# The heads' stage of a hybrid streaming step: masks written behind the last low part of the first gates' weights, the values' low parts on VectorE, signs on ScalarE

## The chip, the core and the metric

The kernel runs on one core of a Trainium2 chip. The metric is the device time in microseconds (us) of one execution. The engines are TensorE (PE, with its weight loads PEld), VectorE (DVE), ScalarE (ACT), GpSimd (POOL) and SyncE (SP), whose queue issues nearly all transfers.

## The reference

One layer of an encoder for a prompt of 1024 rows and a sample of 64 rows, all in float32. The normalised input goes through one projection, whose columns are split among all groups:

```python
z = xn @ w_in
qa, ka, va, qi, ki, wi, qb, kb, vb, ga, gb = jnp.split(z, SPLIT_POINTS, axis=-1)
```

Two mixers of 8 heads of 64 stand side by side. Mixer A lets each query see only the 256 keys with the best index score (48 in the sample):

```python
s = jax.nn.relu(jnp.einsum('bqhd,bsd->bqhs', q_i, ki_all))
isc = jnp.einsum('bqh,bqhs->bqs', w, s).astype(jnp.float32)
isc = jnp.where(vis[None], isc, -jnp.inf)
_, idx = lax.top_k(isc, topk)
```

Mixer B is a band of the query's own chunk of 64 and the eight before it, with a learned bias. Both are projected, weighted by sigmoid gates from `ga` and `gb`, added, projected, and followed by an MLP.

## The kernel before

**Numbers in two parts.** A float32 operand is split into a high part that PE takes (`hi`, a copy on ACT, L123) and a low part (`lo`, raw minus high). `split` (L143) puts the subtraction on DVE (L146) or on POOL (L148). A product is then three matmuls (high by high, high by low, low by high: L154 to L156), or two (L162, L163) where one side is already exact in stacked form (the sample's rows `xsT`, the index scores `s`).

**Stages.** First come normalisation, index keys and queries, and the index scores: `stage_scores(i)` computes the eight heads' scores of row block i on PE into PSUM banks `s`, and DVE adds them up into `work[i]` (L364, L366). Then `project_heads` (L433) makes the six projections of the heads in the order vb, kb, qb, ka, va, qa. Each first loads eight weight pieces of 128 x 512 (transfer `wraw`, high part `whi`, low part `wlo`, 11 buffers each) and then runs 9 units: for each block of 128 rows 24 matmuls of 512 columns, and for the sample's rows 16. A unit's sum in PSUM is copied to a tile `t` (3 buffers), normed and rotated where it must be (POOL L460 and L220 to L223), split into a tile `pair` (3 buffers) and written out (`keep`, `values_to_dram`, `rows_to_dram`, L417 and L424). The sample's two halves are added at L212 (`fold`).

**Order of the stages.** The generator `heads` is drawn one unit at a time. `stage_scores(NT - 1, ...)` draws one behind head 3 and one behind head 7 of the last prompt block, `stage_scores(NT, ...)` one behind head 7 of the sample's block. The rest follows in one loop once the score banks are given back and made into four `wide` banks (L516). Which bank a unit uses is set by `turn`: the first FIRST (3) draws take `acc` (2 banks), later ones acc, wide, wide in turn. The program as a whole is ordered by a compile-time scheduler that simulates the engines; `tc.issue_after(x)` holds what stands under it behind instruction x.

**The masks.** `choose` (L520) finds, in a search of 31 steps, the threshold of each row of blocks 2 to 7: counts on DVE for blocks 2 to 4 (L531), sign sums on ACT for blocks 5 to 7 (L536). Then come `thr` (L570) and a loop over the six blocks (384 to 1024 columns): the scores' signs are given back (L575), scores over the threshold marked and counted (L576, L577), those equal to it marked (L578), their running number made by a scan (L579), cut at what is still needed (L581) and added (L583), and POOL writes the mask (L584). The tiles `seen` have two buffers, so a block's L578 waits for the mask of the block before.

**Gates and attention.** Behind the heads, eight weight pieces of the first four gate blocks are loaded (L633 to L639, low part on DVE), and 12 gate chunks run on PE (L586 to L594), each copied by ACT to one of two `gate` buffers and written out. Then the pools `tk`, `pj`, `works`, `fw` are closed, and the space that they leave is used for the ring of weights that the attention reads beside its own work (`raw`, `hi`, `lo`, L652) and for the attention's tiles. Attention reduces the scores on DVE (L679), takes exponentials on ACT (L683), scales on POOL (L686) and transposes on PE (L699); the mixer's b heads run first, and the masks are first needed when the a heads begin.

Of the kernel before, what the change touches and what calls it, by code (L numbers as in the profile page):

```python
# [14 lines left out]
AF = mybir.ActivationFunctionType  # L15
ALU = mybir.AluOpType
# [10 lines left out]
HD = 64  # L27
# [5 lines left out]
RING = 5  # L33
FIRST = 3
WARM = 18
# [9 lines left out]
def kernel(  # L45
# [97 lines left out]
    def split(raw, hi, lo, lo_on_vector=False):  # L143
        copy(hi, raw)
        if lo_on_vector:
            nc.vector.tensor_sub(lo, raw, hi)  # L146
        else:
            nc.gpsimd.tensor_sub(lo, raw, hi)  # L148
# [275 lines left out]
    def values_to_dram(t, rows, dst, r0):  # L424
        both = pj.tile([P, TP], F32R, tag="pair", name="pair", bufs=3).rearrange("p (h z d) -> p h z d", h=H, z=2)
        split(t[:rows].rearrange("p (h d) -> p h d", d=HD), both[:rows, :, 0], both[:rows, :, 1])
        nc.sync.dma_start(dst[r0:r0 + rows], both.bitcast(F32)[:rows])
# [54 lines left out]
    stage_scores(NT - 1, {3: heads, 7: heads})  # L482
    stage_scores(NT, {7: heads})
    close_pool("ix")
# [34 lines left out]
    def choose(vector, scalar):  # L519
# [50 lines left out]
        nc.vector.tensor_mul(thr, bits.bitcast(F32), sgn)  # L570
        for j, (i, w) in enumerate(zip(blocks, ws)):
            n = w.shape[1]
            over, same = (tk.tile([P, TP], BF16, tag="seen", name="seen", bufs=2) for _ in range(2))
            nth = tk.tile([P, TP], F32, tag="nth", name="nth", bufs=1)
            nc.vector.tensor_scalar(w, w, col(sgn, j), None, op0=ALU.mult)  # L575
            nc.vector.tensor_scalar(over[:, :n], w, col(thr, j), 0.0, op0=ALU.is_gt, op1=ALU.add, accum_out=col(cnt, j))  # L576
# [6 lines left out]
            nc.vector.tensor_add(over[:, :n], over[:, :n], same[:, :n])  # L583
            nc.gpsimd.tensor_scalar(mask[i], over[:, :n], -1.0, BIG, op0=ALU.add, op1=ALU.mult)  # L584

    def gate(m, ws, after=None):  # L586
# [35 lines left out]
    with tc.issue_after(state["last"].ins):  # L622
# [4 lines left out]
        nc.vector.tensor_scalar(mask_s, work_s, 0.5 * (HIDDEN + TAKEN), -BIG, op0=ALU.is_gt, op1=ALU.mult)  # L627
        choose([2, 3, 4], [5, 6, 7])
    todo = [(mix, h) for mix in "ba" for h in range(H)]
    first_head = load_head(*todo[0], kv)  # L630
    for g in range(0, EARLY, 4):
        ws = []
        for k in range(KB):  # L633
# [4 lines left out]
            split(raw, hi, lo, lo_on_vector=True)  # L638
            ws.append((hi, lo))  # L639
        for q in range(4):  # L640
            gate(g + q, [(h[:, q * P:(q + 1) * P], l[:, q * P:(q + 1) * P]) for h, l in ws])
    for nm in ("tk", "pj", "works", "fw"):
        close_pool(nm)
# [688 lines left out]
```

## Time and profile before

| | us |
|---|---|
| median of 3 runs | 1738.48 (1738.3 to 1742.39) |
| the profiled execution | 1739.78 |
| its span, from the first to the last instruction | 1738.0 |
| PE busy | 1709.3 (98%) |
| DVE busy | 1199.3 (69%) |
| ACT busy | 956.4 (55%) |
| POOL busy | 481.4 (28%) |

The mean granted clock of PE is 0.997 of full speed. Busy shares are averages over stages: an engine that is busy for little of the span can still be the one that PE waits for in one place. Times of single instructions below are counted from the start of the span, in the one profiled execution.

### The profile page before, as it was taken

What the parts mean: (1) busy time and instruction counts of PE and PEld (TensorE: products, weight loads), DVE (VectorE), ACT (ScalarE), POOL (GpSimd) and SP (SyncE); (2) the same over time, 40 slices, a digit from 0 to 9 for tenths busy, and PEclk for the clock granted to TensorE, in tenths of its full rate; (3) what the DMA queues carried; (4) which work ended last, traced back from release to release, by engine and by line L of the source; (5) the groups of instructions that cost most, each with busy time, mean ns of one, the idle gap of its engine ahead of it and who ended that gap; (6) DMA issues with size and microseconds to landing.
All of it is one profiled execution on the core that took longest, in us unless ns stands there. A gap on an engine that the chain in (4) does not pass through costs nothing.

```text
span 1738.0 us, 30914 instructions
## 1 busy us (share of the span) xinstructions
PE 1709.3 (98%) x10540; PEld 1551.3 (89%) x10540; DVE 1199.3 (69%) x2765; ACT 956.4 (55%) x1994; POOL 481.4 (28%) x549
## 2 busy tenths in 40 slices
PE   8999999999999999999999999999999999999999
PEld 6877888877999999999999999999999978888887
DVE  6776799994447777774354345865587658868787
ACT  5785889722357777776443346644454447343430
POOL 2252432545424333332344354000000011111122
PEclk9999999999999999999999999999999999999999
DMA  5022475444667876664544559555566589565643
GB/s 175 8 81 104 149 201 151 152 161 161 180 162 191 198 176 153 159 146 134 170 137 136 185 163 284 168 184 183 186 209 204 165 300 316 183 199 149 199 124 103
DMA packets 277197, 294.97 MB, mean 170 GB/s; under 512 B 39792, under 2 KB 201584, under 8 KB 277040
## 3 DMA queue, kind: packets, MB, share of 16 engines
q1 hardware_dynamic: 248064, 257.61, 51.0%
q10 hardware_dynamic: 28976, 35.40, 5.8%
q8 instruction: 83, 1.36, 0.3%
q14 instruction: 74, 0.61, 0.1%
HBM read 199.85 MB, written 93.08 MB: 169 GB/s over the span
## 4 chain that ended last, share of the span: by engine, by line
PE 85%; DVE 6%; DMA 3%; issue 3%; ACT 2%; POOL 1%; SPq 0%; ACTq 0%; DVEq 0%; POOLq 0%
PE acc L154 9%; PE acc L156 9%; PE acc L155 9%; PE x L156 5%; PE x L155 5%; PE x L154 5%; PE pt L699 4%; PE wide L154 3%; PE wide L155 3%; PE wide L156 3%; PE s L162 3%; PE po L715 2%; PE s L163 2%; PE po L714 2%; PE pg L156 2%
## 5 line engine op out<-in xcount | busy, mean ns | idle before, releaser
L155 PE MATMUL x<-lo,hi 128*128 128x512 f32 x432 | 168.8, 391 | 2.3 <-POOL lo L148 1.7
L156 PE MATMUL x<-hi,lo 128*128 128x512 f32 x432 | 166.8, 391 | 0.0
L154 PE MATMUL x<-hi 128*128 128x512 f32 x432 | 164.2, 392 | 0.0
L148 POOL TENSOR_TENSOR lo<-wr,hi 128x512 fp32r<-128x512 f32 x15 | 35.1, 2343 | 455.6 <-ACT hi L123 455.6
L148 POOL TENSOR_TENSOR lo<-raw,hi 128x512 fp32r<-128x512 f32 x88 | 117.9, 1350 | 153.7 <-ACT hi L123 145.8
L123 ACT ACTIVATE hi<-raw 128x512 fp32r<-128x512 f32 x104 | 64.3, 627 | 90.4 <-PE acc L155 21.6
L711 DVE TENSOR_TENSOR pl<-pt,ph 128x512 fp32r<-128x512 f32 (+4 forms) x184 | 96.6, 545 | 19.5 <-ACT ph L123 18.9
L536 ACT ACTIVATE nth<-work,cand 128x768 bf16<-128x768 f32 (+2 forms) x93 | 96.6, 1039 | 18.3 <-DVE cand L553 14.1
L146 DVE TENSOR_TENSOR lo<-hr,hi 128x512 fp32r<-128x512 f32 x108 | 81.6, 756 | 28.9 <-ACT hi L123 28.7
L155 PEld LDWEIGHTS x<-lo,hi 128*128 128x128 f32 x432 | 81.1, 188 | 21.2 <-POOL lo L148 2.1
L123 ACT ACTIVATE ph<-pt 128x512 fp32r<-128x512 f32 (+4 forms) x184 | 81.6, 483 | 32.4 <-PE pt L699 25.6
L156 PEld LDWEIGHTS x<-hi,lo 128*128 128x128 f32 x432 | 81.1, 188 | 17.9
L154 PEld LDWEIGHTS x<-hi 128*128 128x128 f32 x432 | 81.1, 188 | 17.6
L154 PE MATMUL acc<-xnT,hi 128*128 128x384 f32 (+1 forms) x288 | 95.5, 331 | 0.0
L156 PE MATMUL acc<-xnT,lo 128*128 128x384 f32 (+1 forms) x288 | 94.3, 327 | 0.0
L155 PE MATMUL acc<-xnT,hi 128*128 128x384 f32 (+1 forms) x288 | 94.3, 327 | 0.0
L686 POOL TENSOR_SCALAR mw<-mw,sm 128x640 f32<-128x640 f32 (+1 forms) x64 | 56.7, 886 | 131.8 <-DVE sm L685 131.7
L154 PE MATMUL wide<-whi,xnT 128*128 128x512 f32 x224 | 89.4, 404 | 1.7 <-DVE work_s L366 1.7
L156 PE MATMUL wide<-whi,xnT 128*128 128x512 f32 x224 | 90.1, 402 | 0.0
L155 PE MATMUL wide<-wlo,xnT 128*128 128x512 f32 x224 | 89.9, 401 | 0.0
L714 PE MATMUL po<-ph,vhl 128*128 128x256 f32 (+2 forms) x336 | 86.0, 274 | 0.4 <-ACT ph L123 0.4
L715 PE MATMUL po<-pl,vhl 128*128 128x256 f32 (+2 forms) x336 | 85.9, 285 | 0.6 <-DVE pl L711 0.6
(671 smaller groups left out, 5963.2 us busy)
## 6 DMA issues: line engine op xcount, KB each, us to landing
hr<-h SPq DMA_DIRECT2D x108, 256.0 KB, 3.6
wr<-in_w_down_dram SPq DMA_DIRECT2D x76, 256.0 KB, 4.0
wraw<-in_w_in_dram SPq DMA_DIRECT2D x56, 256.0 KB, 2.8
h<-h ACTq DMA_DIRECT2D x32, 272.0 KB, 2.1
raw<-in_w_out_dram SPq DMA_DIRECT2D x32, 256.0 KB, 3.0
raw<-in_w_up_dram SPq DMA_DIRECT2D x32, 256.0 KB, 3.5
out_dram<-t SPq DMA_DIRECT2D x24, 256.0 KB, 2.4
g_dram<-gate SPq DMA_DIRECT2D x32, 192.0 KB, 3.2
```

The lines of the kernel that those rows point to most:

```text
L123: return nc.scalar.activation(out, in_, AF.Copy)
L146: nc.vector.tensor_sub(lo, raw, hi)
L148: nc.gpsimd.tensor_sub(lo, raw, hi)
L154: nc.tensor.matmul(out, sh, mh, start=(opens and i == 0), stop=False, skip_group_check=resumes)
L155: nc.tensor.matmul(out, sh, ml, start=False, stop=False, skip_group_check=resumes)
L156: last = nc.tensor.matmul(out, sl, mh, start=False, stop=(closes and i == n - 1), skip_group_check=resumes)
L536: nc.scalar.activation(sign[:, :w.shape[1]], w, AF.Sign, bias=against, scale=-1.0, accum_out=col(cnt, j))
L686: nc.gpsimd.tensor_scalar(m[:rows, :n], m[:rows, :n], sm[:rows, 6:7], 1.0, op0=ALU.mult, op1=ALU.mult)
L699: nc.tensor.transpose(ps[:krows, oo:oo + qrows], m[:qrows, kc:kc + krows], ident[:qrows, :qrows])
L711: nc.vector.tensor_sub(pl[:kr, a:b], ps[:kr, a:b], ph[:kr, a:b])
L714: nc.tensor.matmul(dst, vhl[:krows, vt, :], ph[:krows, oo:oo + width], start=(idx == 0), stop=False)
L715: nc.tensor.matmul(dst, vhl[:krows, vt, :], pl[:krows, oo:oo + width], start=False, stop=(idx == n - 1))
```

## The change

Five edits. FIRST goes from 3 to 5, so that the first five units drawn use `acc`. `stage_scores(NT, ...)` draws a unit behind head 3 too. The low parts of the values va are made on DVE, not on POOL (vb stays on POOL). The six multiplications that give the scores back their signs become ACT copies with a scale. The rest of the mask loop becomes a function `mask_out(j)`, which is called for the six blocks behind the gates, under `tc.issue_after` of the low part of the eighth weight piece of the first gates.

```diff
--- before.py
+++ after.py
@@ -31,7 +31,7 @@
 DFF = 4096
 EPS = 1e-6
 RING = 5
-FIRST = 3
+FIRST = 5
 WARM = 18
 BIG = 1e30
 HIDDEN = -2.0e38
@@ -143,7 +143,7 @@
     def split(raw, hi, lo, lo_on_vector=False):
         copy(hi, raw)
         if lo_on_vector:
-            nc.vector.tensor_sub(lo, raw, hi)
+            last["lo"] = nc.vector.tensor_sub(lo, raw, hi)
         else:
             nc.gpsimd.tensor_sub(lo, raw, hi)
 
@@ -423,7 +423,8 @@
 
     def values_to_dram(t, rows, dst, r0):
         both = pj.tile([P, TP], F32R, tag="pair", name="pair", bufs=3).rearrange("p (h z d) -> p h z d", h=H, z=2)
-        split(t[:rows].rearrange("p (h d) -> p h d", d=HD), both[:rows, :, 0], both[:rows, :, 1])
+        split(t[:rows].rearrange("p (h d) -> p h d", d=HD), both[:rows, :, 0], both[:rows, :, 1],
+              lo_on_vector=dst is v_dram["a"])
         nc.sync.dma_start(dst[r0:r0 + rows], both.bitcast(F32)[:rows])
 
     def keep(nm, t, rows, i):
@@ -480,7 +481,7 @@
 
     heads = project_heads()
     stage_scores(NT - 1, {3: heads, 7: heads})
-    stage_scores(NT, {7: heads})
+    stage_scores(NT, {3: heads, 7: heads})
     close_pool("ix")
 
     masks = open_pool("masks")
@@ -568,11 +569,14 @@
         nc.vector.scalar_tensor_tensor(cand.bitcast(F32), low, 1.5 * 2.0 ** -24, low, op0=ALU.mult, op1=ALU.add)
         nc.vector.copy_predicated(bits, ok, cand)
         nc.vector.tensor_mul(thr, bits.bitcast(F32), sgn)
-        for j, (i, w) in enumerate(zip(blocks, ws)):
+        for j, w in enumerate(ws):
+            nc.scalar.activation(w, w, AF.Copy, scale=col(sgn, j))
+
+        def mask_out(j):
+            i, w = blocks[j], ws[j]
             n = w.shape[1]
             over, same = (tk.tile([P, TP], BF16, tag="seen", name="seen", bufs=2) for _ in range(2))
             nth = tk.tile([P, TP], F32, tag="nth", name="nth", bufs=1)
-            nc.vector.tensor_scalar(w, w, col(sgn, j), None, op0=ALU.mult)
             nc.vector.tensor_scalar(over[:, :n], w, col(thr, j), 0.0, op0=ALU.is_gt, op1=ALU.add, accum_out=col(cnt, j))
             nc.vector.tensor_scalar(col(need, j), col(cnt, j), -1.0, float(TOPK_P), op0=ALU.mult, op1=ALU.add)
             nc.vector.tensor_scalar(same[:, :n], w, col(thr, j), None, op0=ALU.is_equal)
@@ -582,6 +586,8 @@
                                            op0=ALU.is_le, op1=ALU.mult)
             nc.vector.tensor_add(over[:, :n], over[:, :n], same[:, :n])
             nc.gpsimd.tensor_scalar(mask[i], over[:, :n], -1.0, BIG, op0=ALU.add, op1=ALU.mult)
+
+        return mask_out
 
     def gate(m, ws, after=None):
         for c0, n in CHUNKS:
@@ -625,7 +631,7 @@
             nc.vector.max(out=m8, in_=work_s)
             nc.vector.match_replace(out=work_s, in_to_replace=m8, in_values=work_s, imm_value=TAKEN)
         nc.vector.tensor_scalar(mask_s, work_s, 0.5 * (HIDDEN + TAKEN), -BIG, op0=ALU.is_gt, op1=ALU.mult)
-        choose([2, 3, 4], [5, 6, 7])
+        mask_out = choose([2, 3, 4], [5, 6, 7])
     todo = [(mix, h) for mix in "ba" for h in range(H)]
     first_head = load_head(*todo[0], kv)
     for g in range(0, EARLY, 4):
@@ -637,8 +643,13 @@
             lo = pj.tile([P, 512], F32R, tag="wlo", name="wlo", bufs=11)
             split(raw, hi, lo, lo_on_vector=True)
             ws.append((hi, lo))
+        lows = last["lo"]
         for q in range(4):
             gate(g + q, [(h[:, q * P:(q + 1) * P], l[:, q * P:(q + 1) * P]) for h, l in ws])
+
+        with tc.issue_after(lows.ins):
+            for j in range(6):
+                mask_out(j)
     for nm in ("tk", "pj", "works", "fw"):
         close_pool(nm)
```

How the order of instructions changes, at three places. First PE at the last score block (`s`, the sample's rows); `acc` and `wide` are projection units. Before:

```order
L162 MATMUL s<-kih,qiT 64x192
L163 MATMUL s<-kil,qiT 64x192
L162 MATMUL s<-kih,qiT 64x192
L163 MATMUL s<-kil,qiT 64x192
L154 MATMUL wide<-whi,xnT 128x512
L155 MATMUL wide<-wlo,xnT 128x512
L156 MATMUL wide<-whi,xnT 128x512
L154 MATMUL wide<-whi,xnT 128x512
```

After:

```order
L162 MATMUL s<-kih,qiT 64x192
L163 MATMUL s<-kil,qiT 64x192
L162 MATMUL acc<-whi,xsT 128x512
L163 MATMUL acc<-wlo,xsT 128x512
L162 MATMUL acc<-whi,xsT 128x512
L163 MATMUL acc<-wlo,xsT 128x512
L162 MATMUL s<-kih,qiT 64x192
L163 MATMUL s<-kil,qiT 64x192
L154 MATMUL acc<-whi,xnT 128x512
L155 MATMUL acc<-wlo,xnT 128x512
L156 MATMUL acc<-whi,xnT 128x512
L162 MATMUL s<-kih,qiT 64x192
```

Before, the eight pairs of narrow matmuls follow on each other and `wide` comes behind them; after, `acc` matmuls stand between the pairs.

Second DVE, at the masks. `thr` is the threshold, `work_111` the scores of the first block (384 columns), `t` tiles of a projection. Before, the masks follow `thr` at once:

```order
L139 TENSOR_TENSOR nt<-nt,ms 128x8
L139 TENSOR_TENSOR nt<-nt,ms 64x8
L569 COPY_PREDICATED bits<-ok,cand 128x6
L140 SCALAR_TENSOR_TENSOR rs<-nt,r_3703 128x8
L140 SCALAR_TENSOR_TENSOR rs<-nt,r_3758 64x8
L570 TENSOR_TENSOR thr<-bits,sgn 128x6
L457 TENSOR_TENSOR t<-wide,rs 128x512
L457 TENSOR_TENSOR t<-fold,rs 64x512
L576 TENSOR_SCALAR seen,cnt<-work_111,thr 128x384
L578 TENSOR_SCALAR seen<-work_111,thr 128x384
L577 TENSOR_SCALAR need<-cnt 128x1
L579 SCALAR_TENSOR_TENSOR nth<-ones,seen 128x384
```

After, they begin behind the last `wlo` of the first gates' weights, with small steps of the last tile of qa between them:

```order
L458 TENSOR_TENSOR t<-wide,rs 128x512 x2
L454 TENSOR_REDUCE ss<-t 64x8
L146 TENSOR_TENSOR wlo<-wraw,whi 128x512
L580 TENSOR_SCALAR seen,cnt<-work_111,thr 128x384
L582 TENSOR_SCALAR seen<-work_111,thr 128x384
L130 TENSOR_SCALAR ms<-ss 64x8
L132 RECIPROCAL r_4675<-sd 64x8
L581 TENSOR_SCALAR need<-cnt 128x1
L583 SCALAR_TENSOR_TENSOR nth<-ones,seen 128x384
L138 SCALAR_TENSOR_TENSOR nt<-r_4675 64x8
```

and the last block (`work_116`, 1024 columns) is followed by the attention's first reduction (L690 of the changed file, L679 before):

```order
L580 TENSOR_SCALAR seen,cnt<-work_116,thr 128x1024
L582 TENSOR_SCALAR seen<-work_116,thr 128x1024
L581 TENSOR_SCALAR need<-cnt 128x1
L583 SCALAR_TENSOR_TENSOR nth<-ones,seen 128x1024
L585 SCALAR_TENSOR_TENSOR seen<-nth,need,seen 128x1024
L587 TENSOR_TENSOR seen<-seen 128x1024
L690 ISA m,sm<-s,turned 128x128
L690 ISA sm 128x1
L690 ISA m,sm<-s,turned 128x256
```

The masks have moved from before the units of va to behind the weights of the gates, in front of the attention.

Third SP's queue at the start of the attention's ring of weights (`raw`); `g_dram<-gate` are the writes of gate chunks, `qT_a` those of the last queries. Before, behind the third gate write:

```order
L594 DMA g_dram<-gate 128x384 x2
L594 DMA g_dram<-gate 128x320
L652 DMA raw<-in_w_in_dram 128x4x128 x3
L422 DMA qT_a_60<-pair 128x4x128
L422 DMA qT_a_61<-pair 128x4x128
L594 DMA g_dram<-gate 128x384
L422 DMA qT_a_60<-pair 128x4x128
L422 DMA qT_a_61<-pair 128x4x128
L652 DMA raw<-in_w_in_dram 128x4x128 x2
```

After, behind the seventh:

```order
L600 DMA g_dram<-gate 128x384
L422 DMA qT_a_60<-pair 128x4x64
L422 DMA qT_a_61<-pair 128x4x64
L600 DMA g_dram<-gate 128x384
L600 DMA g_dram<-gate 128x320
L600 DMA g_dram<-gate 128x384
L663 DMA raw<-in_w_in_dram 128x4x128 x3
L600 DMA g_dram<-gate 128x384
L663 DMA raw<-in_w_in_dram 128x4x128 x2
```

The first `raw` has moved from behind three gate writes to behind seven.

## Rows read from the trace of the kernel before

**Rows 1.** From the page of the profile: the first line of its part 1 (busy us, share of the span, instructions of each engine), of its part 4 (the chain that ended last, by engine), one group of its part 5 (line, engine, operation, operands and count; busy us in all and mean ns of one; idle time before them) and one line of its part 6 (DMA issues: count, KB each, us to landing).

```profile
PE 1709.3 (98%) x10540; PEld 1551.3 (89%) x10540; DVE 1199.3 (69%) x2765; ACT 956.4 (55%) x1994; POOL 481.4 (28%) x549
...
PE 85%; DVE 6%; DMA 3%; issue 3%; ACT 2%; POOL 1%; SPq 0%; ACTq 0%; DVEq 0%; POOLq 0%
...
L536 ACT ACTIVATE nth<-work,cand 128x768 bf16<-128x768 f32 (+2 forms) x93 | 96.6, 1039 | 18.3 <-DVE cand L553 14.1
...
g_dram<-gate SPq DMA_DIRECT2D x32, 192.0 KB, 3.2
```

**Rows 2.** What PE waits for, from 95 to 200 us. Columns: engine, tile and line, the releaser; us in all, times, the longest.

```profile
PE wide L154 <- DVE work_s L366: 1.7, 1, 1.7
```

**Rows 3.** PE in the order of time, from 150 to 160 us. Columns: start, us, engine, line, operation, out<-in, shapes; in brackets the idle time before it and what ended it. A matmul's duration is longer than its distance from the next, since matmuls are pipelined.

```profile
150.22 0.25 PE L162 MATMUL s<-kih,qiT 128*64 128x192 f32 x1
...
150.84 0.25 PE L163 MATMUL s<-kil,qiT 128*64 128x192 f32 x1
151.54 0.30 PE L162 MATMUL s<-kih,qiT 128*64 128x192 f32 x1 [0.45 <-DVE work_s L364]
...
153.08 0.31 PE L162 MATMUL s<-kih,qiT 128*64 128x192 f32 x1
...
155.14 0.51 PE L154 MATMUL wide<-whi,xnT 128*128 128x512 f32 x1 [1.66 <-DVE work_s L366]
...
157.14 0.63 PE L154 MATMUL wide<-whi,xnT 128*128 128x512 f32 x1
...
159.59 0.39 PE L154 MATMUL wide<-whi,xnT 128*128 128x512 f32 x1
```

**Rows 4.** What PE waits for, from 325 to 500 us, columns as in rows 2.

```profile
PE acc L154 <- ACT whi L123: 4.4, 2, 3.2
PE acc L155 <- POOL wlo L148: 1.1, 1, 1.1
```

**Rows 5.** PE in the order of time, from 384 to 402 us, and the first matmul of the gates, columns as in rows 3. From the first row up to the fifth, without it, there are 41 matmuls of 512 columns.

```profile
384.51 0.40 PE L156 MATMUL acc<-whi,xnT 128*128 128x512 f32 x1
...
386.48 0.40 PE L154 MATMUL wide<-whi,xnT 128*128 128x512 f32 x1
...
388.11 0.39 PE L155 MATMUL wide<-wlo,xnT 128*128 128x512 f32 x1
...
397.97 0.50 PE L154 MATMUL acc<-whi,xnT 128*128 128x512 f32 x1 [3.20 <-ACT whi L123]
...
401.95 0.39 PE L155 MATMUL acc<-wlo,xnT 128*128 128x512 f32 x1
...
440.37 0.34 PE L154 MATMUL acc<-xnT,whi 128*128 128x384 f32 x1
```

**Rows 6.** The chain that ended last, in the order of time, from 380 to 500 us. Columns: start, us, engine, tile and line.

```profile
379.82 2.98 DVE nth L579
...
395.57 0.61 DVE fold L212
...
397.40 0.53 ACT whi L123
```

**Rows 7.** Two stretches of 5 us. Columns: the stretch, its length, busy us and count of PE, of PE's weight loads, of DVE, ACT and POOL, the granted PE clock, the share of the DMA engines, GB/s.

```profile
155.00:160.00 5.00, 4.86 (x14) 3.89 (x15) 5.00 (x17) 0.00 (x0) 0.69 (x4) 0.66 0.24 62
...
370.00:375.00 5.00, 5.00 (x25) 3.88 (x24) 5.00 (x9) 1.23 (x2) 0.73 (x1) 1.00 0.54 147
```

**Rows 8.** DVE in the order of time: pieces of the mask loop, the eighth low part of the gates' weights (L146) and the first reduction of the attention (L679). Columns as in rows 3.

```profile
357.22 0.60 DVE L576 TENSOR_SCALAR_CACHE_REDUCE seen<-work,thr 128x384 bf16<-128x384 f32 x1
...
361.73 0.75 DVE L576 TENSOR_SCALAR_CACHE_REDUCE seen<-work,thr 128x512 bf16<-128x512 f32 x1
...
363.49 0.79 DVE L578 TENSOR_SCALAR seen<-work,thr 128x512 bf16<-128x512 f32 x1 [0.82 <-POOL mask L584]
...
366.96 0.88 DVE L576 TENSOR_SCALAR_CACHE_REDUCE seen<-work,thr 128x640 bf16<-128x640 f32 x1
...
373.58 1.76 DVE L579 TENSOR_TENSOR_SCAN nth<-ones,seen 128x768 f32<-128x768 f32 x1
...
386.72 1.71 DVE L578 TENSOR_SCALAR seen<-work,thr 128x1024 bf16<-128x1024 f32 x1
...
447.40 0.68 DVE L146 TENSOR_TENSOR wlo<-wraw,whi 128x512 fp32r<-128x512 f32 x1
...
491.00 0.29 DVE L679 CUSTOM_DVE_ANT_0 m<-s,turned 128x128 f32<-128x128 f32 x1 [26.10 <-POOL turned L507]
```

**Rows 9.** POOL in the order of time: the start of a stretch of rotary work, two values' low parts in a row (x2), and three low parts of the attention's weights in a row (x3). Columns as in rows 3.

```profile
356.84 2.97 POOL L460 TENSOR_TENSOR t<-t,g_ka 128x512 f32<-128x512 f32 x2 [7.99 <-DVE t L457]
...
389.52 4.97 POOL L148 TENSOR_TENSOR pair<-t,pair 128x512 fp32r<-128x512 f32 x2
...
462.13 3.78 POOL L148 TENSOR_TENSOR lo<-raw,hi 128x512 fp32r<-128x512 f32 x3 [3.80 <-ACT hi L123]
```

**Rows 10.** ACT in the order of time: the high part of the first weight of the attention's ring, the load of the exponential's table, the first exponential. Columns as in rows 3.

```profile
461.42 0.63 ACT L123 ACTIVATE hi<-raw 128x512 fp32r<-128x512 f32 x1 [1.87 <-DMA raw<-in_w_in_dram]
...
491.23 1.28 ACT L683 ACT_TABLE_LOAD   x1
492.53 0.40 ACT L683 ACTIVATE m<-m,sm 128x128 f32<-128x128 f32 x1
```

**Rows 11.** SP's queue in the order of time: the issue of the ring's first three weight transfers. Columns: start, us over all, queue, line, operation, out<-in, count.

```profile
458.36 1.49 SPq L652 DMA_DIRECT2D raw<-in_w_in_dram  x3
```

## The prediction

> **What bounds the kernel now.** First the page: TensorE (PE) is busy 98% of the span and holds 85% of the chain that ended last [rows 1]. In the stage of the heads' projections and first gates, from about 155 to 490 us, PE nearly always has a next matmul ready, so only two things can move the time: an idle stretch of PE that goes, or one that comes. So the next view is what PE waits for.
>
> From 95 to 200 us it is mostly VectorE (DVE), adding up the last score block: 1.7 us before the first `wide` matmul [rows 2]. In the order of time, eight pairs of narrow score matmuls stand alone from 150.22, the later ones (151.54 to 153.08 is three of them) 0.51 us apart because each waits for DVE to give back a score bank, and the first `wide` matmul comes at 155.14 [rows 3]. In the slice from 155 to 160 us the granted clock is 0.66, from 370 to 375 us 1.00 [rows 7]: after the thin stretch PE runs for some 3 us at the lower of its two levels (1.2 and 2.4 GHz), a `wide` matmul then taking 0.63 us instead of 0.39 [rows 3, 5].
>
> From 325 to 500 us PE waits 5.5 us for pieces of weights, twice for a high part on ACT and once for a low part on POOL [rows 4]. They lie between 384.51 and 401.95 [rows 5]. The chain says why: while DVE makes the masks, its scan (L579) and, behind the masks, the sample rows' addition (L212) are on the path, and a weight's high part comes after these at 397.40 [rows 6]. ACT works in order: its copies of weights stand behind copies of the values' tiles, which need a `pair` buffer that POOL's low part frees. Two such low parts take 4.97 us there, against 3.78 us for three of the same size beside an idle DVE [rows 9].
>
> **What the change removes.** *First loss.* PE's pitch at full clock is (388.11 - 386.48)/7 = 0.233 us for a 512-column matmul [rows 5] and (150.84 - 150.22)/7 = 0.089 for a narrow one [rows 3]. From 150.22 to 159.59 stand 16 narrow and 12 wide: 16 x 0.089 + 12 x 0.233 = 4.22 us of work in 9.37 us, a loss of 5.15 us. With FIRST at 5 and a projection unit drawn at head 3 of the last score block too, the order of PE has three or four `acc` matmuls between the narrow pairs and fifteen more of them before the first `wide` one. DVE needs 0.51 us a head; PE then spends 3 or 4 x 0.233 + 2 x 0.089 = 0.9 to 1.1 us on one, so DVE keeps up. I take the whole 5.15 as gained, and as bound below that the 1.7 us wait stays, with its slow clock, which leaves about 2.
>
> The price is that the last score comes some 6 us later, so the search for the thresholds that follows on DVE and ACT ends about 6 us later. PE waits for nothing of that search; it shares DVE and ACT with PE's weights.
>
> *Second loss.* From 384.51 to 401.95 there are 41 matmuls of 512 columns, 41 x 0.233 = 9.57 us of work in 17.44 us: 7.87 us lost. With the mask loop gone from there, DVE has 31 us less to do, L212 is no longer behind it, and the values' low parts leave POOL. Ten of these move to DVE at about 0.68 us, the low part of the same size at 447.40 [rows 8]: 6.8 us on a DVE that is rid of 31. The chain of ACT copy, low part, transfer and next buffer gets shorter, so I take the 7.87 as gained whole. Bound: if ACT alone is too slow, the 3.2 us wait and the slow clock behind it stay, 5 of the 7.87.
>
> *Signs.* Six multiplies leave DVE and become ACT copies with a scale. ACT's nearest operation, the sign pass with a column as operand, takes 1.04 us at 768 to 1024 columns [rows 1], so the six (384 to 1024) take at most 6.2 us and by length about 5. ACT is busy 1.23 of 5 us about there [rows 7]. That cover makes the cost 0; without it the next weights' high parts come up to 6 us later once, and what PE has in stock then decides.
>
> Sum of the gains: 5.15 + 7.87 = 13.0 us.
>
> **What it adds.** The masks now run on DVE behind the low part that stands at 447.40, 7.0 us after the gates' PE work began at 440.37 [rows 5, 8], and DVE's next work after them is the attention's first reduction. Before, DVE sat idle there for 26.1 us up to 491.00 [rows 8], 50.6 us after the gates' start; that idle time is the cover. Two things queue behind the masks.
>
> (1) DVE itself. From the first mask operation to the end of the last comparison took 386.72 + 1.71 - 357.22 = 31.2 us [rows 8]. In it 0.8 us is a wait for POOL's write of a mask, 1.8 us are transposed tiles' low parts, and I put 2.7 us to stretching beside POOL (the 896 scan takes 2.98 [rows 6], by length from the 768 one's 1.76 [rows 8] it would be 2.05; other steps alike): 26 remain. In the new place 3.8 us of other DVE work stands in between by the order (one tile's scaling and small steps, three low parts). So about 29.5 us from the end of that low part, 7.6 us after the start: the comparison ends at 37 us, the masks some 5 us later. DVE itself is not late for 50.6.
>
> (2) The attention's weights. Their first transfer on SP (`raw`) waits for that last comparison, since its buffer lies over released tiles; before, it was issued at 458.36 [rows 11], 18 us after the start. The way from it to the first exponential: landing 3.06 (458.36 to 461.42) [rows 10, 11], copy 0.63 [rows 10], two low parts of 1.26 on POOL [rows 9], a second landing and copy 3.69, the copy of a gate 0.5, which stands behind that `hi` on ACT, its write's landing 3.2 [rows 1] because gates have two buffers, the last gate's copy 0.44, table load 1.28 [rows 10]: 15.3, with the gaps between engines 15.7 us. The exponential is then at 37 + 15.7 = 52.7 us after the start; before, it was at 492.53 - 440.37 = 52.2 [rows 5, 10]. So 0.5 us late, and I add 1 us for mask writes that now stand behind POOL's rotary steps, on which the next block's comparison waits. PE has nothing else there and loses it one to one: 1.5 us. Bounds: 0 (the comparison 2 us earlier), and 7.4: the masks at the old stretched rate, 31.2 + 2.0 + 1.5 = 34.7, put the comparison at 42.3 and the exponential 5.8 us late, and the slow clock after such a wait costs about 1.6 more, as the ten matmuls from 397.97 did (3.98 us instead of 2.33) [rows 5].
>
> What contention does there the trace shows in little: the first mask block ran beside 6 us of POOL's rotary work from 356.84 [rows 9] and took 361.73 - 357.22 = 4.5 us, the larger second one without its wait 366.96 - 361.73 - 0.82 = 4.4 [rows 8]. About 1 us was lost in 6. The Trainium skill (SBUF — State Buffer, "Who interferes with whom") says that a VectorE instruction with two SBUF inputs contends with a GpSimd one that reads SBUF, and the later one fully blocks. By that rule in full force the whole of POOL's rotary work, not a sixth, could fall on DVE; rival (b) is that case.
>
> Net: 13.0 - 1.5 = 11.5 us. The profiled execution took 1739.78 us (span 1738.0), 1.3 above the median of 1738.48. 1739.78 - 11.5 = 1728.3, and against the median **1727.0 us**; 1725.5 if the handover is free.
>
> **Rivals.** (a) *The handover to the attention is dear.* For it: the first `raw` is behind a long chain on DVE, among POOL's rotary steps. Against it: 26.1 us of idle DVE. At the bound of 7.4 us the gain is 5.6, the time 1732.9; in the middle, at 4 us, 1729.5. (b) *DVE and POOL block each other in full:* the 6 us and more of rotary work, say 8, come on the comparison, 8 + 1.5 us on the exponential, 1.6 of slow clock; gain 1.9, time 1736.6, no change. Against it the 1 in 6 above. (c) *One loss stays.* ACT, with the signs and a later search before it, is still late for the weights: gain 13.0 - 5 - 1.5, time 1732.0, or with all of the second loss 1734.8. For it: the search ends nearer the values' unit; against it: 31 us of DVE work left that place. (d) *Slower.* The mask work takes over 42 us from the low part instead of 29.5. Then the comparison ends 50 us after the start, the chain of 15.7 us behind it puts the exponential past 65, and the 13 us that PE waits eat both gains; each further microsecond is lost, at 50 us of mask work 8 of them: 1746. Against it: the same work took 31.2 us where DVE and POOL were both at their busiest. (e) *The change doesn't do what it says.* The order shows masks, signs and low parts moved, so it does.
>
> **How the numbers follow.** Forecast 0.62 (its own range 1724.5 to 1729.5), (a) 0.18, (b) 0.05, (c) 0.10, (d) 0.05, (e) 0. The range for 8 in 10 runs from 1723.0 (free handover and some 2 us of spread between runs) to 1733.5, which holds (a) and most of (c). 0.3%, 5.2 us, is about what a measurement of this kernel can tell from no change: faster, below 1733.3, has 0.86, within it 0.09, slower 0.05.
>
> **What would show it.** Right: no wait of PE for DVE and a granted clock of 1.00 from 150 to 165 us; no wait of PE for `whi` or `wlo` in the values' unit; the gates' first matmul some 13 us earlier; the mask lines behind the eighth low part of the gates' weights; the exponential 52 to 54 us after the gates' start. Wrong: PE waiting over 3 us at the attention's first transposes with the table load behind a late copy of a gate, or the same `whi` waits at the values' unit with ACT busy on signs.

## The result, and the profile after

The changed kernel takes 1730.38 us (median of 4 runs, 1730.19 to 1730.58), the kernel before 1739.95 in the same comparison (4 runs, 1738.3 to 1742.39): ratio 0.9944, 95% interval 0.9927 to 0.9961, so 9.6 us are gained where 11.5 were forecast. The forecast time was 1727.0; of the 3.4 us between, 1.5 are the median of the kernel before, which was 1738.48 when the forecast was made. The span of the profiled execution fell from 1738.0 to 1728.4 us.

The same two lines of the page as in [rows 1]: busy time by engine, and the chain that ended last.

```profile
PE 1705.5 (99%) x10540; PEld 1550.1 (90%) x10540; DVE 1201.6 (70%) x2769; ACT 961.7 (56%) x2000; POOL 466.7 (27%) x539
...
PE 75%; DVE 4%; DMA 3%; issue 2%; POOL 1%; ACT 1%; SPq 0%; ACTq 0%; DVEq 0%; POOLq 0%
```

PE is busy for 3.8 us less than before with the same 10540 matmuls, and 99% of the span: what went were idle stretches and slow matmuls.

What PE waits for, first from 95 to 200 us (compare [rows 2]), then from 195 to 430, then from 325 to 500 us (compare [rows 4]); columns: what waited, the releaser; us in all, times, the longest.

```profile
...
PE s L162 <- DVE work L366: 0.2, 1, 0.2
```

```profile
PE pt L411 <- DVE pair L417: 1.7, 1, 1.7
```

```profile
PE pt L710 <- POOL m L697: 1.1, 2, 0.9
```

Both waits of before are gone: none for the score sums (`work`, `work_s`) above 0.2 us, none for `whi` or `wlo` from 195 us on. A new one stands there, 1.7 us for a low part of kb's transposed tiles (L417), and the wait for the first probabilities has grown from 0.2 us to 1.1 (L697 is L686 of before).

Slices of 5 us (columns as in [rows 7]):

```profile
155.00:160.00 5.00, 5.00 (x28) 3.97 (x26) 2.21 (x5) 2.66 (x6) 1.29 (x1) 1.00 0.40 157
...
395.00:400.00 5.00, 5.00 (x23) 4.00 (x23) 4.06 (x17) 2.94 (x7) 0.00 (x0) 1.00 0.35 105
...
245.00:250.00 5.00, 5.00 (x20) 3.96 (x20) 4.89 (x18) 4.72 (x11) 0.00 (x0) 0.74 0.86 229
```

The granted clock is 1.00 from 155 to 160 us, where it was 0.66. The low stretch now stands elsewhere, 0.74 from 245 to 250 us.

**The last score block.** PE in the order of time there, and the first matmul of the gates (compare [rows 3, 5]):

```profile
150.68 0.25 PE L162 MATMUL s<-kih,qiT 128*64 128x192 f32 x1
...
150.86 0.41 PE L155 MATMUL acc<-wlo,xnT 128*128 128x512 f32 x1
...
162.80 0.39 PE L154 MATMUL wide<-whi,xnT 128*128 128x512 f32 x1
...
431.08 0.34 PE L154 MATMUL wide<-xnT,whi 128*128 128x384 f32 x1
```

From 150.68 to 162.80 stand 16 narrow and 45 wide matmuls, 16 x 0.089 + 45 x 0.233 = 11.9 us of work in 12.12 us. The 5.15 us lost there before are down to 0.2.

**The stall at the end of kb.** PE, DVE and POOL in the order of time, in three fences:

```profile
241.68 0.40 PE L155 MATMUL wide<-wlo,xnT 128*128 128x512 f32 x1
243.75 0.43 PE L411 MATMUL pt<-ident,t 64*128 64x64 f32 x4 [1.68 <-DVE pair L417]
244.11 0.79 PE L156 MATMUL wide<-whi,xnT 128*128 128x512 f32 x1
...
247.25 0.54 PE L154 MATMUL wide<-whi,xnT 128*128 128x512 f32 x1
```

```profile
237.68 1.26 DVE L561 TENSOR_TENSOR ok<-cnt,lim 128x6 int32<-128x6 f32 x1
...
238.98 1.23 DVE L562 COPY_PREDICATED bits<-ok,cand 128x6 int32<-128x6 int32 x1
...
240.91 0.61 DVE L532 TENSOR_SCALAR_CACHE_REDUCE seen<-work,cand 128x384 bf16<-128x384 f32 x1
...
242.92 0.69 DVE L417 TENSOR_TENSOR pair<-pt,pair 128x512 fp32r<-128x512 f32 x1
```

```profile
237.63 1.30 POOL L461 TENSOR_TENSOR t<-t,g_kb 128x512 f32<-128x512 f32 x1 [1.73 <-DMA wraw<-in_w_in_dram]
238.89 1.29 POOL L148 TENSOR_TENSOR wlo<-wraw,whi 128x512 fp32r<-128x512 f32 x1
```

PE wants to transpose the sample's rows of kb from 241.9 on and needs the PSUM bank that the low part at 242.92 gives back at 243.61. The high part that it subtracts was ready on ACT at 240.32; the low part comes later because it stands on DVE behind three counts of the search (the first is at 240.91), and these behind two tiny steps (`ok`, L561, and the copy of `bits`, L562) that take 1.26 and 1.23 us where they otherwise take 0.17. They end at 238.94 and 240.21, just when the POOL steps that began beside them end (237.63 + 1.30 and 238.89 + 1.29). From 241.68 to 247.63 PE does nine wide matmuls and four small ones, 2.46 us of work in 5.95: 3.5 us are lost, 1.8 in the wait and 1.7 at the lower clock behind it (0.43 us a matmul).

In the kernel before, the same low part with a step of the search ahead of it, and the same transposes, DVE and then PE:

```profile
240.26 1.24 DVE L553 TENSOR_SCALAR cand<-bits 128x6 int32<-128x6 int32 x1
...
242.74 0.69 DVE L417 TENSOR_TENSOR pair<-pt,pair 128x512 fp32r<-128x512 f32 x1
```

```profile
244.86 0.46 PE L411 MATMUL pt<-ident,t 64*128 64x64 f32 x4
```

DVE gave the bank back at 243.43, nearly the same moment, but PE came 2.9 us later and found it free. In that kernel, too, a tiny step (L553) took 1.24 us ahead of the low part, and two counts stood between them; so stretched steps and counts ahead of the low part are not new, and what is new is that PE is there first.

**The handover to the attention.** DVE, SP, ACT and PE in the order of time, in four fences (compare [rows 8, 10, 11]), and PE in the kernel before in a fifth:

```profile
437.49 0.69 DVE L146 TENSOR_TENSOR wlo<-wraw,whi 128x512 fp32r<-128x512 f32 x1 [0.19 <-ACT whi L123]
438.10 0.60 DVE L580 TENSOR_SCALAR_CACHE_REDUCE seen<-work,thr 128x384 bf16<-128x384 f32 x1
...
445.03 2.19 DVE L583 TENSOR_TENSOR_SCAN nth<-ones,seen 128x512 f32<-128x512 f32 x1
...
466.26 0.75 DVE L582 TENSOR_SCALAR seen<-work,thr 128x1024 bf16<-128x1024 f32 x1
```

```profile
467.07 1.48 SPq L663 DMA_DIRECT2D raw<-in_w_in_dram  x3
...
472.57 1.62 SPq L663 DMA_DIRECT2D raw<-in_w_in_dram  x2
```

```profile
470.11 0.63 ACT L123 ACTIVATE hi<-raw 128x512 fp32r<-128x512 f32 x1 [4.39 <-DMA raw<-in_w_in_dram]
...
481.51 0.44 ACT L123 ACTIVATE gate<-acc 128x320 f32<-128x320 f32 x1 [2.74 <-DMA g_dram<-gate]
481.97 1.28 ACT L694 ACT_TABLE_LOAD   x1
483.27 0.40 ACT L694 ACTIVATE m<-m,sm 128x128 f32<-128x128 f32 x1
```

```profile
480.33 0.22 PE L162 MATMUL s<-kh,qT 128*128 128x128 f32 x1
...
484.57 0.33 PE L710 MATMUL pt<-ident,m 128*128 128x128 f32 x1 [0.93 <-POOL m L697]
```

```profile
490.52 0.22 PE L162 MATMUL s<-kh,qT 128*128 128x128 f32 x1
...
493.83 0.33 PE L699 MATMUL pt<-ident,m 128*128 128x128 f32 x1
```

The masks begin behind the eighth low part at 438.10 and the last comparison ends at 467.01; SP issues the ring's first transfer 0.06 us later, at 467.07, having waited 5.1 us for that comparison. The chain from there went nearly as forecast: landing and `hi` at 470.11, second transfers at 472.57, the last gate's copy at 481.51, the table load, and the exponential at 483.27. The gates' PE work starts at 431.08, 9.3 us earlier than before, and ends at 480.33, 10.2 us earlier; PE then waits 0.93 us for the first probabilities and transposes them 9.3 us earlier than before (484.57 and 493.83).

### The profile page after: what moved, and what is told of

The parts are those of the page before. It is cut to its first block, busy times and chain, and to the rows that moved or that the text cites. A ratio compares the mean times of both kernels' runs of the same rounds, so it can differ in the third digit from the quotient of the medians.

```text
span 1728.4 us, 30917 instructions
## 1 busy us (share of the span) xinstructions
PE 1705.5 (99%) x10540; PEld 1550.1 (90%) x10540; DVE 1201.6 (70%) x2769; ACT 961.7 (56%) x2000; POOL 466.7 (27%) x539
## 4 chain that ended last, share of the span: by engine, by line
PE 75%; DVE 4%; DMA 3%; issue 2%; POOL 1%; ACT 1%; SPq 0%; ACTq 0%; DVEq 0%; POOLq 0%
PE acc L154 7%; PE acc L156 7%; PE acc L155 7%; PE x L155 5%; PE x L156 5%; PE x L154 5%; PE pt L710 4%; PE wide L156 2%; PE po L726 2%; PE wide L154 2%; PE wide L155 2%; PE s L162 2%; PE po L725 2%; PE s L163 2%; PE pg L156 2%; PE pe L156 2%
## 5 line engine op out<-in xcount | busy, mean ns | idle before, releaser
L148 POOL TENSOR_TENSOR lo<-wr,hi 128x512 fp32r<-128x512 f32 x15 | 40.0, 2667 | 456.0 <-ACT hi L123 456.0
L156 PE MATMUL wide<-whi,xnT 128*128 128x512 f32 x256 | 102.0, 401 | 0.0
L155 PE MATMUL wide<-wlo,xnT 128*128 128x512 f32 x256 | 101.7, 400 | 0.0
L154 PE MATMUL wide<-whi,xnT 128*128 128x512 f32 x256 | 101.0, 400 | 0.0
L146 DVE TENSOR_TENSOR lo<-hr,hi 128x512 fp32r<-128x512 f32 x108 | 81.3, 755 | 26.5 <-ACT hi L123 26.3
L697 POOL TENSOR_SCALAR mw<-mw,sm 128x640 f32<-128x640 f32 (+1 forms) x64 | 56.7, 887 | 131.9 <-DVE sm L696 129.3
```

The source lines that it names most:

```text
L146: last["lo"] = nc.vector.tensor_sub(lo, raw, hi)
L154: nc.tensor.matmul(out, sh, mh, start=(opens and i == 0), stop=False, skip_group_check=resumes)
L155: nc.tensor.matmul(out, sh, ml, start=False, stop=False, skip_group_check=resumes)
L156: last = nc.tensor.matmul(out, sl, mh, start=False, stop=(closes and i == n - 1), skip_group_check=resumes)
L697: nc.gpsimd.tensor_scalar(m[:rows, :n], m[:rows, :n], sm[:rows, 6:7], 1.0, op0=ALU.mult, op1=ALU.mult)
```

## The experiments

Each has its own runs of the kernel before beside it; ratios are to these, with 95% intervals.

**The first part alone.** The kernel before with

```diff
-FIRST = 3
+FIRST = 5
...
-    stage_scores(NT, {7: heads})
+    stage_scores(NT, {3: heads, 7: heads})
```

> The kernel before with only FIRST at 5 and the extra unit drawn at head 3 of the last score block; masks, signs and the values' low parts stay where they were. Theory: this part alone removes the 5.1 us loss at the last score block and alone brings the new stall at the end of kb (PE waits 1.7 us for DVE's low part L417 at 243.75 in the changed kernel, 3.4 us with the slow clock behind it), because both come from drawing units earlier and so starting the threshold search later: 1739.9 - 5.1 + 3.4 = 1738.2, or a little more if the masks, now later, hold the qa weights longer. Rival: the kb stall belongs to another part of the change (the order that the scheduler finds): then 1734.8 and no wait at L411.

1738.99 us against 1740.69, ratio 0.9993 (0.9984 to 1.0003). What PE waits for, from 95 to 200 us, 200 to 325, and 325 to 500 (one, one, and three lines):

```profile
PE s L162 <- DVE work L366: 0.3, 2, 0.2
...
PE pt L411 <- DVE pair L417: 1.8, 1, 1.8
...
PE wide L155 <- DVE wlo L146: 5.0, 2, 3.6
PE wide L155 <- POOL wlo L148: 2.1, 1, 2.1
PE wide L154 <- ACT whi L123: 0.4, 1, 0.4
```

The loss at the score block is gone and the wait at kb is there, 1.8 us, so both belong to this part. The waits at the qa weights are 7.5 us in all where they were 5.5; the threshold is ready 12 us later there (`thr` at 368.02, before at 355.93), so the masks lie beside other weights, and that this makes the difference is likely but not tested. By itself this part gains nothing that can be told.

**All but the first part.** The changed kernel with FIRST at 3 and a unit at head 7 only.

```diff
-FIRST = 5
+FIRST = 3
...
-    stage_scores(NT, {3: heads, 7: heads})
+    stage_scores(NT, {7: heads})
```

> The changed kernel with FIRST back at 3 and one unit at head 7 of the last block. Theory: the loss at the last score block is back (1.7 us wait, 5.1 in all), the kb stall is gone, the waits for whi and wlo between 384 and 402 stay gone, and the handover to the attention costs 0.5 to 1.5 us: 1739.9 - 7.9 + 1 = 1733. Rival: the values' unit needed the shifted search too; then a wait for whi of over 1 us is left and the time is 1735 or more.

1732.99 us, ratio 0.9959 (0.9945 to 0.9974). PE's waits, from 95 to 200 us (first line) and 325 to 500:

```profile
PE wide L154 <- DVE work_s L366: 1.7, 1, 1.7
...
PE pt L710 <- POOL m L697: 1.1, 2, 0.9
PE pt L411 <- POOL t L223: 1.1, 1, 1.1
PE pt L411 <- DVE pair L417: 1.0, 1, 1.0
```

No wait for `whi` or `wlo`, none at kb: the second gain and the first are separate, and the stall at kb goes with the first. Two waits came that nobody had expected, at the transposes of qa's last tiles in the gates: one for POOL's rotary steps, which now lie beside the masks, and one for a low part on DVE, where the masks are made.

**The values' low parts back on POOL.**

```diff
-        split(t[:rows].rearrange("p (h d) -> p h d", d=HD), both[:rows, :, 0], both[:rows, :, 1],
-              lo_on_vector=dst is v_dram["a"])
+        split(t[:rows].rearrange("p (h d) -> p h d", d=HD), both[:rows, :, 0], both[:rows, :, 1])
```

> The changed kernel with the values' low parts back on POOL. Theory: the masks were what held ACT and DVE; with them gone POOL's 1.3 us low parts are fast enough and nothing comes back: 1730.4, within 0.5. Rival: the pair buffers are still the limit of ACT's queue, a wait for whi of 1 us or more returns at the qa weights and the time is 1732 or more.

1730.49 us, ratio 0.9946 (0.9931 to 0.9961), no wait at the qa weights: once the masks are away, this edit changes nothing that can be told.

**The signs back on DVE.**

```diff
-            nc.scalar.activation(w, w, AF.Copy, scale=col(sgn, j))
+            nc.vector.tensor_scalar(w, w, col(sgn, j), None, op0=ALU.mult)
```

> The changed kernel with the six sign multiplies back on DVE at the end of the search. Theory: they are off PE's path on either engine: 1730.4, within 0.5, and no wait of PE over 0.3 us between 330 and 400. Rival: 3.4 us more on DVE in front of the values' work delay a fold or a low part, and a wait for whi or wlo of over 0.5 us appears.

1729.97 us, ratio 0.9942 (0.9927 to 0.9957). A wait for `whi` of 0.9 us did come, at 335.70, which the expectation put on the rival's side; the time does not show it. In the profiled execution PE waited 1.8 us at kb as in the changed kernel, and ran at full pitch behind it.

**The masks alone.** The kernel before with only the mask loop moved, the sign multiply of each block on DVE at the end of the search:

```diff
-        for j, (i, w) in enumerate(zip(blocks, ws)):
+        for j, w in enumerate(ws):
+            nc.vector.tensor_scalar(w, w, col(sgn, j), None, op0=ALU.mult)
+
+        def mask_out(j):
...
+        with tc.issue_after(lows.ins):
+            for j in range(6):
+                mask_out(j)
```

> The kernel before with only the masks moved behind the gates' weights, the sign multiplies still on DVE where the search ends; FIRST 3, the values' low parts on POOL. Theory: this one edit is the whole of the second loss, since neither the signs nor the values' low parts changed the time when undone alone: as the changed kernel with FIRST back at 3, 1733, with no wait for whi or wlo between 380 and 405. Rival: each of the two could stand in for the other; without both, waits of ACT or POOL at the qa weights return, 1735 or more.

1733.72 us, ratio 0.9969 (0.9957 to 0.9981). PE's only large wait from 325 to 500 us:

```profile
PE pt L411 <- POOL t L223: 2.2, 2, 1.7
```

No wait at the qa weights. So the place of the masks is the second gain, and neither companion is needed for it; as in the kernel without the first part, waits for rotary steps beside the masks take back some of it.

**kb without its gain.** A look at the stall: POOL's multiply of kb by its gain left out.

```diff
-                    if gn != "qb":
+                    if gn not in ("qb", "kb"):
```

> The changed kernel without the multiplication of kb by its gain (POOL, nine times 1.3 us); kb is left unscaled, so the keys of mixer B are not the reference's. PE's order is the same up to the kb stall. Theory: the stall at the sample rows of kb is POOL's doing: its gain multiply and a weight's low part hold up two tiny steps of the search on DVE (1.26 and 1.23 us where they take 0.16), and the low part that PE waits for stands behind them. Without the gain multiply at least one of the two is back at 0.16 and PE's wait of 1.7 us goes under 0.8. Rival: it is the place of L417 behind three counts in DVE's order alone; then the wait stays at 1.5 us or more.

1730.36 us in one run. No wait of PE above 0.2 us from 200 to 325 us, so the stall is gone. But the time is the same: 1.0 us for a low part of a weight and two waits of 0.4 stand at 330 to 357 us, and 1.4 us at the handover. The tiny steps of the search took 0.34 us and less from 230 us on, and the low part came at 236.37, in front of the counts and not behind them, since DVE's order changed with the edit. So the run doesn't tell whether the blocked steps or the place of the low part made the stall.

**Masks early.** The changed kernel with the masks held only behind qa's last low part on DVE.

```diff
+    qa_low = last["lo"]
...
-        with tc.issue_after(lows.ins):
+        with tc.issue_after(qa_low.ins):
```

> The changed kernel with the mask steps held only behind the last low part of qa's weights on DVE, some 40 us earlier, not behind the gates' weights. Theory of the handover: the wait of 0.9 us for the first probabilities (and 1.5 us in all behind it) is due to the attention's ring, whose first load waits for the 1024 block's comparison; early masks free it, the exponential stands again 52 us after the gates' start, and 1.0 to 1.5 us are gained: 1729.0. Rival 1: the handover is late for another reason, and the wait stays: 1730.4. Rival 2: masks beside qa's weights hold up their low parts as before the change: a wait for wlo of over 1 us and 1731 or more.

1731.84 us, ratio 0.9959 (0.9945 to 0.9974). PE's waits from 325 to 500 us:

```profile
PE pt L411 <- POOL t L223: 2.2, 1, 2.2
PE pt L710 <- POOL m L697: 0.2, 1, 0.2
```

The handover's wait is gone down to the 0.2 us of before, as the theory said: it was the ring's wait for the last comparison. But the masks now lie beside qa's rotary steps on POOL, and a wait of 2.2 us for these takes its place. The wait for weights of the second rival didn't come either; a third thing did.

**Low parts of qb's weights on DVE,** four of eight, with early masks and without:

```diff
-                split(raw, hi, lo, lo_on_vector=nm in ("va", "qa") and k % 2 == 0)
+                split(raw, hi, lo, lo_on_vector=nm in ("qb", "va", "qa") and k % 2 == 0)
```

> As the kernel with early masks, and four of the eight low parts of qb's weights on DVE, not on POOL. Theory: fewer of POOL's long steps meet the search's tiny steps at the end of kb, so the 3.4 us stall there shrinks: 1727 or less, with the wait at L411 under 0.8 us. Rival: DVE, which is the search's bound there, gets 2.7 us more work just in front of the low part that PE waits for, and the wait stays or grows: 1729 or more.

1732.13 us, ratio 0.9958 (0.9943 to 0.9972). The wait at kb is 0.7 us, with the clock at 1.00 behind it, but 1.8 us for a low part at qa's transposes, 1.7 for low parts of the gates' weights and 1.1 for rotary steps came behind it.

> The changed kernel with four of the eight low parts of qb's weights on DVE. Theory: the kb stall shrinks as it did in the kernel with early masks (PE's wait at the sample rows of kb 0.7 us in place of 1.7), about 2.5 us with the slow clock are gained, and the masks' place costs what it cost: 1728. Rival: the shift by a few microseconds puts another wait at qa or the gates' weights, and the time is 1730 or more.

1729.15 us, ratio 0.9937 (0.9920 to 0.9954): the wait at kb is 0.5 us, the one at the handover 1.4, one of 0.7 for a `whi` and one of 0.5 for rotary steps at the gates. The interval covers the changed kernel's ratio, so it can't be called better. Nor does it show what the theory said: two tiny steps of the search were still blocked for 1.3 and 1.2 us there, and three counts still stood ahead of the low part, which at last waited 0.6 us for its high part on ACT. The bank came free at 243.58, as in the changed kernel (243.61); PE came to the transposes 1 us later, by another order.

**FIRST at 6, with early masks; FIRST at 4.**

```diff
-FIRST = 5
+FIRST = 6
```

> As the kernel with early masks, with FIRST at 6. The sixth unit takes the narrow banks too, which changes the order of PE at the end of kb. Theory: the kb stall is a meeting of a few microseconds and not a bound of DVE as a whole, so another order can miss it: 1726, no wait at L411. Rival: DVE is short of time in kb as a whole, and the stall comes back somewhere in kb: 1729 or more.

1741.27 us, ratio 1.0011 (1.0002 to 1.0020), the whole gain lost: PE waits 2.6 us for the gain multiply in kb and, from 335 us on, 3.1 for rotary steps, 1.8 for L417 and 3.8 for weights. The wait at L417 in kb is gone, but a stall in kb is back in another form, as the rival said, and more of them further on.

```diff
-FIRST = 5
+FIRST = 4
```

> The changed kernel with FIRST at 4: the fifth unit takes a wide bank, so four or five of the narrow score pairs stand alone again behind the first three. Theory: about half of the first loss comes back (2 to 3 us at the last score block, with or without the slow clock), the search starts earlier by some 3 us, and the kb stall, a meeting of POOL's steps with the search's, goes or changes: between 1728 and 1733. Rival: the stall at kb stays at 3 us and the first loss comes back as well: 1733 or more.

1736.69 us, ratio 0.9984 (0.9975 to 0.9993): a time that the rival allows, but not for its reason. The wait of 1.7 us for `work_s` came back, the stall at kb fell to 0.9 us, two waits of 0.8 us for weights came (at 225 and 340 us), and the handover became dear. SP's issues of the ring, ACT's copy of its fifth piece, and PE's first transpose of probabilities:

```profile
470.89 1.49 SPq L663 DMA_DIRECT2D raw<-in_w_in_dram  x3
...
477.64 6.30 SPq L663 DMA_DIRECT2D raw<-in_w_in_dram  x3
...
482.81 0.63 ACT L123 ACTIVATE hi<-raw 128x512 fp32r<-128x512 f32 x1 [0.64 <-DMA raw<-in_w_in_dram]
...
490.47 1.20 PE L710 MATMUL pt<-ident,m 128*128 128x128 f32 x3 [3.84 <-POOL m L697]
```

The last comparison ended at 470.83, 36.9 us after the gates' start at 433.95, 1 us more than in the changed kernel (35.9). The ring's fifth transfer went out 6.75 us behind the first in both (477.64 here, 473.82 there), but its copy on ACT began 5.2 us after that issue and not 3.6 (482.81; 477.38 there); the copies of the last gates come behind it, and the exponential came 55.2 us after the start: 3.8 us of waiting. Why the landing took longer is open.

**The sample's own top-k late.** Six rounds of MAX8 and MATCH_REPLACE moved from the start of the search to behind qa's low parts:

```diff
-    with tc.issue_after(state["last"].ins):
+    with tc.issue_after(qa_low.ins):
         for _ in range(TOPK_S // 8):
...
+    with tc.issue_after(state["last"].ins):
+        mask_out = choose([2, 3, 4], [5, 6, 7])
```

> The changed kernel with the sample's own top-k (six rounds of MAX8 and MATCH_REPLACE, some 0.7 us each on DVE, and one compare), which stands at 161 to 172 us between the first search steps, held behind the last low part of qa's weights on DVE. Theory: PE, 5 us earlier through the first part of the change, has overtaken DVE, which is busy 98% from 220 to 240 us with the search and kb's own steps; DVE reaches the low part that the sample's transposes need at 243.6 in the changed kernel and at 243.4 in the kernel before. With 4 us less of work in front DVE reaches it 2 to 4 us earlier, the wait of 1.7 us goes under 0.5, and the time is 1727.5. Rival: only the meeting of two tiny steps with POOL's long ones makes the wait; those are not touched, the wait stays at 1.5 us or comes back elsewhere in kb, 1730. A second rival: the six rounds now hold up the low parts of qa's or the gates' weights, a wait for wlo appears, 1730 or more.

1733.41 us, ratio 0.9961 (0.9947 to 0.9975). DVE ahead of the same low part, and the low part:

```profile
235.99 1.25 DVE L139 TENSOR_TENSOR nt<-nt,ms 128x8 f32<-128x8 f32 x1
...
239.16 1.28 DVE L140 SCALAR_TENSOR_TENSOR rs<-nt,r 64x8 f32<-64x8 f32 x1
...
240.52 1.68 DVE L458 TENSOR_TENSOR t<-fold,rs 64x512 f32<-64x512 f32 x1
...
244.53 0.69 DVE L417 TENSOR_TENSOR pair<-pt,pair 128x512 fp32r<-128x512 f32 x1
```

The low part comes at 244.53, later and not earlier, and PE waits 2.1 us. So the theory that DVE's load as a whole sets this place is not borne out. The 4 us taken away did not bring the search forward: the result of its first step (`ok`) came at 174.30 us, against 174.42 in the changed kernel, since DVE now waited 2.4 us for ACT's counts there, and that of the eleventh at 240.36, against 237.68. PE's transposes still meet three counts. Three more steps are stretched there, to 1.25, 1.28 and 1.68 us. Waits of 1.2 to 1.4 us for kb's gain multiply, for rotary steps and at the handover came besides.

## Why the prediction was right, and where it was not

**First loss, 5.15 us.** Right: 0.2 is left, and the clock stays up.

**The price of the later search, taken as nothing.** This is the step that failed: "PE waits for nothing of that search; it shares DVE and ACT with PE's weights." The search did end some 7 us later (`thr` at 363.20 and 355.93), as the prediction put it. But PE does wait for DVE steps that stand among the search's, the low parts of transposed tiles. PE had come forward, DVE had not, and at the end of kb 3.5 us of the 5.15 were given back. The first part alone shows both, and the kernels without it show neither. Shown is that the stall belongs to this part, that PE arrives 2.9 us earlier at a bank that comes free at the same moment, and that it vanishes without POOL's gain multiply, in another order of DVE. Not settled is how much of it is the two blocked steps of the search and how much the place of the low part behind three counts: each edit that touched it also changed the order, and an edit that moves this low part alone was not run.

**Second loss, 7.87 us.** Right in cause, and in size as far as the runs tell it: no wait for weights is left, and the masks alone do it. All but the first part gained 7.7 us; the masks alone gained 5.9 (3.3 to 7.5), with 2.2 us of waiting for rotary steps among it. The two companions, credited with part of the cover, were not needed; costs of 0 for them were right.

**The handover, 1.5 us.** Right in mechanism and near in size: comparison 35.9 us after the gates' start (forecast 37), 28.9 us of masks (29.5), chain to the exponential 16.3 us (15.7), exponential at 52.2 (52.7). Of the 1 us added for mask writes, one wait of 0.35 us shows. PE lost 0.9 us against before: its first transposes stand 4.24 us behind the attention's first matmul, 3.31 before. That the exponential stands at the same 52.2 as before and PE still waits has a reason that I missed: a group of eight transposes now lies before the gates and not in them, so the gates' PE work is 0.9 us shorter (49.25 and 50.15 us).

The sum by what was measured: 5.15 - 0.2 + 7.87 - 3.5 - 0.9 = 8.4 us, against 9.6 in the spans. Of the 1.2 us between, 0.9 come ahead of the attention, which PE reaches 10.2 us earlier where the first four terms make 9.3, and 0.3 behind its first transposes (9.3 us earlier there, 9.6 at the end); what they are was not traced. So it is in part luck that the gain came within 1.9 us of the forecast though a cost of 3.5 had been put at nothing: the handover cost 0.6 less than forecast, and 1.2 us came from elsewhere. The sign that hung on that cost failed: the gates' first matmul came 9.3 us earlier, not 13.

Rival (a), the dear handover, is what FIRST at 4 showed, in another order. Rival (b), the full block of DVE and POOL, was the truer reading of single steps, see below; as a cost at the handover it did not come (28.9 us of masks).

## What to carry to other kernels

When an engine that leads is freed in one place, look for the next place where it meets an engine that was not freed: the buffer there comes free when it did before, and the gain is given back up to that moment. Ask of a moved step not only whether its work is hidden, but which queue's wait its last instruction ends, and count the chain behind that. In an order found by simulation, a table's number moved by one can cost most of what the whole edit brings (FIRST at 4) or all of it (FIRST at 6, with early masks), so the neighbours of a value belong to the measurement.

## What the runs showed that I had not expected

**DVE behind POOL.** Steps of 128 x 6 elements that take 0.17 us took 1.26 and 1.23 us in the changed kernel and ended within 0.03 us of the end of the POOL step beside them. That agrees with the rule of the Trainium skill (SBUF — State Buffer, "Who interferes with whom") that the later of the two fully blocks until the first has finished, where the prediction held it to be a part only. In the long mask steps the loss looks to be of the same kind: the 512-column scan at 445.03 took 2.19 us beside POOL and 1.21 to 1.23 in seven other runs, and it ended 1.1 us after the POOL step that had begun before it (444.66 to 446.13).

**The clock after a wait.** The same wait at kb, 1.7 to 1.8 us, was followed by some 3 us at the lower clock in the changed kernel (0.74 from 245 to 250 us), with the first part alone, with the values' low parts on POOL (0.68) and with early masks (0.66). In the profiled execution with the signs on DVE none followed (1.00), and none behind the 2.1 us with the sample's top-k late (1.00). What decides it the runs don't show.
